# Rotary embedding on one core: one early load moved to SyncE's queue, one late load split in two

## The chip, the core and the metric

The kernel runs on one core of a Trainium2 chip. It uses all five engines of the core: TensorE (PE in the profile), VectorE (DVE), ScalarE (ACT), GpSimd (POOL) and SyncE (SP), and the 16 DMA engines that move data between HBM and SBUF. The metric is the device time of one execution in microseconds.

## The reference

The input `x` has 16 batches of 512 positions with 1024 numbers each, 16 heads of 64. `cos` and `sin` have one row of 32 numbers for each position.

```python
x = x.reshape(batch, seq, num_heads, head_dim)
x1, x2 = x[..., :half_dim], x[..., half_dim:]
cos = cos[None, :, None, :]
sin = sin[None, :, None, :]
rotated = np.concatenate([x1 * cos - x2 * sin, x1 * sin + x2 * cos], axis=-1)
```

For each head, the first half of the result is `x1*cos - x2*sin` and the second half `x1*sin + x2*cos`. All is float32: 33.55 MB are read and as many written.

## The kernel before

The 8192 positions are cut into 64 units, called rows in the code and here, numbered `u` from 0 to 63. A row is a block of 128 partitions by 1024 numbers (512 KB). Eight rows make a tile (4 MB). There are eight tiles, called tile 1 to tile 8 here; the code numbers them from 0. In SBUF there is a ring of 40 rows, so tiles 1 to 5 have places of their own, and tiles 6, 7 and 8 use those of tiles 1, 2 and 3 again. The result is written over the input in SBUF and stored from there.

`TILES` (L33) has one line for each tile: its rows, its place in the ring, into how many loads and stores it is cut, and the stores that must have landed before it may be loaded. Tile 1 is loaded and stored in two halves of four rows, tile 8 is stored in two halves; all else moves in whole tiles. That makes nine loads and ten stores.

Each row takes two products and one sum:

- VectorE multiplies the row by the cosine into PSUM (`t1_ps`, three buffers, L341).
- The row with its halves swapped is multiplied by the signed sine into `t2_sb` (six buffers), mostly by GpSimd: two rows at once at L308, one row at L165. VectorE takes a few of these rows itself (L165).
- The two are summed. For 45 rows VectorE adds them (L350). For 19 rows TensorE adds `t2_sb` into PSUM by a product with the identity (L268), and ScalarE copies the sum to SBUF (L230).

The engines run in written order, each with its own list of instructions, and wait on semaphores. VectorE multiplies row `u` and then adds row `u - 1`. GpSimd goes ahead of VectorE as far as the six buffers allow. On GpSimd and VectorE the wait for a load stands at the first row of that load (`wait_landed`, L190).

The tables: SyncE loads `sin` and `cos` first (L196). TensorE spreads them over the partitions by small matrix products (L251), ScalarE turns them into the sine table (L220, L221), and only then can VectorE and GpSimd begin.

The queues: all loads of `x` are issued by ScalarE. The six loads of tiles 1 to 5 come first, before anything else that ScalarE does (L208). The loads of tiles 6, 7 and 8 are late loads: they stand in ScalarE's list behind rows 21, 28 and 37 (`BEHIND`, L45), and each waits for the stores whose place it takes (L233). SyncE issues the two tables and then the ten stores, each as soon as its last row is summed (`wait_added`, then L203). At the end SyncE waits for the stores that no load waited for (L204).

Of the kernel before, what the change touches and what calls it, by code (L numbers as in the profile page):

```python
# [6 lines left out]
def bass_split_heads_rope_kernel(  # L7
# [21 lines left out]
    COPY = mybir.ActivationFunctionType.Copy  # L29

    TILES = (  # L33
        (8, 0, (4, 4), (4, 4), ()),
        (8, 8, (8,), (8,), ()),
        (8, 16, (8,), (8,), ()),
        (8, 24, (8,), (8,), ()),
        (8, 32, (8,), (8,), ()),
        (8, 0, (8,), (8,), (0, 1)),
        (8, 8, (8,), (8,), (2,)),  # L40
        (8, 16, (8,), (4, 4), (3,)),
    )
    RING = 40

    BEHIND = {6: 21, 7: 28, 8: 37}  # L45
    first_row = [sum(t[0] for t in TILES[:i]) for i in range(len(TILES))]
    NU = sum(t[0] for t in TILES)
    assert NU * P == batch * seq
# [3 lines left out]

    loads = []
    stores = []
    for t, (n, place, ins, outs, _) in enumerate(TILES):
        assert sum(ins) == n == sum(outs) and place + n <= RING
        loads += [(t, sum(ins[:i]), m) for i, m in enumerate(ins)]
        stores += [(t, sum(outs[:i]), m) for i, m in enumerate(outs)]
    load_at = {(t, o): i for i, (t, o, _) in enumerate(loads)}
    store_after = {first_row[t] + o + m - 1: i for i, (t, o, m) in enumerate(stores)}  # L60
    late = [i for i, (t, _, _) in enumerate(loads) if TILES[t][4]]
    awaited = sorted({k for t in TILES for k in t[4]})


    V_ROWS = {8: (3, 6)}
# [25 lines left out]
    with ExitStack() as stack:  # L91
# [13 lines left out]
        sem_in = [stack.enter_context(nc.semaphore(f"in{i}")) for i in range(len(loads))]  # L105
        sem_out = {k: stack.enter_context(nc.semaphore(f"out{k}")) for k in awaited}
# [39 lines left out]
        def in_dram(flat, t, o, m):  # L146
            n = TILES[t][0]
            run = flat[first_row[t] * P:(first_row[t] + n) * P, :].rearrange("(p r) d -> p (r d)", r=n)
            return run[:, o * dim:(o + m) * dim]

        def place_of(u):
            t, r = rows[u]
            return TILES[t][1] + r

        def in_sbuf(t, o, m):
            k = TILES[t][1] + o
            return x_sb[:, k:k + m].rearrange("p n h t d -> p (n h t d)")
# [14 lines left out]
        def wait_added(eng, u):  # L172
            if n_pe[u]:
                eng.wait_ge(sem_a, n_pe[u])
            if n_comb[u]:
                eng.wait_ge(sem_v, n_comb[u])
# [9 lines left out]
        def load(eng, i):  # L186
            t, o, m = loads[i]
            eng.dma_start(in_sbuf(t, o, m), in_dram(xf, t, o, m)).then_inc(sem_in[i], 16)

        def wait_landed(eng, t, r):  # L190
            if (t, r) in load_at:
                eng.wait_ge(sem_in[load_at[t, r]], 16)

        def on_sync(sp):
            for c, table, sem in ((1, sin, sem_sin), (0, cos, sem_cos)):
                sp.dma_start(stage[:, c, :], table.rearrange("(s r) d -> s (r d)", r=R1)).then_inc(sem, 16)  # L196
            for u in range(NU):
                if u not in store_after:
                    continue
                k = store_after[u]  # L200
                t, o, m = stores[k]
                wait_added(sp, u)
                sp.dma_start(in_dram(of, t, o, m), in_sbuf(t, o, m)).then_inc(sem_out.get(k, sem_rest), 16)  # L203
            sp.wait_ge(sem_rest, 16 * (len(stores) - len(awaited)))  # L204

        def on_scalar(ae):
            early = [i for i in range(len(loads)) if i not in late]
            for i in early:  # L208
                load(ae, i)
            ae.wait_ge(sem_i, 2)  # L210
            for n in SIZES:
                m = n // R1
                ae.activation(  # L213
                    pick[n][:],
                    ident[:].rearrange("q (s k) -> q k s", k=m)[:, :, None, :].broadcast_to([P, m, m, P // m]),
                    COPY,
                ).then_inc(sem_g, 1)
            for i, n in enumerate(SIZES):
                ae.wait_ge(sem_t, i + 1)
                ae.activation(s_sb[n][:, :, 0, :], raw_sin[n], COPY, scale=-1.0)  # L220
                ae.activation(s_sb[n][:, :, 1, :], raw_sin[n], COPY).then_inc(sem_s, 1)  # L221
            for n in SIZES:
                v = V_ROWS[n]
                some = raw_sin[n][:, v[0]:v[-1] + 1:max(1, v[-1] - v[0]), :]
                ae.activation(v_ps[n][:, :, 0, :], some, COPY, scale=-1.0)
                ae.activation(v_ps[n][:, :, 1, :], some, COPY).then_inc(sem_s, 1)
            for u in range(NU):
                if PE2[u]:
                    ae.wait_ge(sem_e, n_pe[u])
                    ae.activation(xs[:, place_of(u), :], t1_ps[:, u % NT1, :], COPY).then_inc(sem_a, 1)  # L230
                for i in late:
                    if BEHIND[i] == u:
                        for j in TILES[loads[i][0]][4]:  # L233
                            ae.wait_ge(sem_out[j], 16)
                        load(ae, i)

        def on_tensor(pe):
            pe.wait_ge(sem_z, 1)
            for k in range(NT1):
                for b in range(EH):  # L240
                    pe.matmul(  # L241
                        t1_ps[:, k, b * BANK:(b + 1) * BANK], zero[:, 0:P], zero[:], start=True, stop=True
                    ).then_inc(sem_w, 1)
            pe.wait_ge(sem_g, len(SIZES))
            pe.wait_ge(sem_cos, 16)
            pe.wait_ge(sem_sin, 16)
            pe.wait_ge(sem_w, NT1 * EH)
            for n in SIZES:
                for c, to in enumerate((c_ps[n], raw_sin[n])):
                    for k in range(n // R1):  # L250
                        ins = pe.matmul(  # L251
                            to[:, k * R1:(k + 1) * R1, :].rearrange("p r d -> p (r d)"),
                            pick[n][:, k].rearrange("q b s -> q (b s)"),
                            stage[:, c, :],
                            start=c == 0,
                            stop=True,
                            skip_group_check=c == 1,
                        )
                ins.then_inc(sem_t, 1)
            for u in range(NU):  # L260
                if not PE2[u]:
                    continue
                if TWO[u - 1]:
                    pe.wait_ge(sem_q[(u - 1) % NT2], made[u - 1])
                pe.wait_ge(sem_q[u % NT2], made[u])
                t2 = t2_sb[:, u % NT2, :, :, :].rearrange("p h t d -> p (h t d)")
                for b in range(EH):
                    ins = pe.matmul(  # L268
                        t1_ps[:, u % NT1, b * BANK:(b + 1) * BANK],
                        ident[:],  # L270
                        t2[:, b * BANK:(b + 1) * BANK],
                        start=False,
                        stop=True,
                        skip_group_check=True,
                    )
                ins.then_inc(sem_e, 1)
# [40 lines left out]
        def on_vector(ve):  # L317
# [39 lines left out]
            for u in range(NU + LEAD):  # L357
# [6 lines left out]
                if u >= LEAD and not ahead and not PE2[u - LEAD]:  # L364
                    comb(u - LEAD)

        on_sync(nc.sync)
        on_scalar(nc.scalar)
        on_gpsimd(nc.gpsimd)
        on_tensor(nc.tensor)  # L370
        on_vector(nc.vector)

# [32 lines left out]
```

## Time and profile before

| what | us |
|---|---|
| median of 3 runs | 161.01 (160.85 to 161.12) |
| profiled execution, its own time | 160.98 |
| its span, first to last instruction | 159.7 |
| VectorE busy | 133.8 (84%) |
| GpSimd busy | 126.3 (79%) |
| TensorE busy | 60.5 (38%) |
| ScalarE busy | 22.1 (14%) |
| share of the 16 DMA engines' time, loads of x (q10) | 49.4% |
| the same, tables and stores (q1) | 49.1% |

The span lies between the first and the last instruction of the program; the time of the execution has some more around it. A transfer has two moments in the profile: its issue by SyncE or ScalarE, and its landing, when its semaphore has counted all of its 16 engines. Between the two it may stand in its queue behind earlier transfers. In what follows, a time without more said is counted from the start of the span.

The cost of the instructions on a row:

```profile
L308 POOL TENSOR_TENSOR t_sb<-x_sb,sine 128x2048 f32<-128x2048 f32 x22 | 99.1, 4526 | 1.6 <-DMA x_sb<-in_x_dram 1.3
L341 DVE TENSOR_TENSOR t_ps<-x_sb,tab_ps 128x1024 f32<-128x1024 f32 x64 | 76.8, 1221 | 14.1 <-PE t_ps L251 12.5
L350 DVE TENSOR_TENSOR x_sb<-t_ps,t_sb 128x1024 f32<-128x1024 f32 x45 | 54.5, 1215 | 1.6 <-POOL t_sb L308 0.9
L230 ACT ACTIVATE x_sb<-t_ps 128x1024 f32<-128x1024 f32 x19 | 19.5, 1024 | 91.5 <-PE t_ps L268 91.5
```

Each line has the busy time of the group and the mean duration in ns of one instruction, and behind the second bar the idle time of the engine just before them and what ended most of it.

### The profile page before, as it was taken

The numbers are of one execution on the slowest core, as the hardware profiler recorded it, in microseconds if no ns is written. First come the engines' busy times: TensorE is split into PE (matmuls) and PEld (weight loads), VectorE is DVE, ScalarE is ACT, GpSimd is POOL, SyncE is SP. The second block draws the span as 40 slices with busy tenths as digits, with TensorE's granted clock in tenths as the row PEclk, the third lists the DMA queues.
The fourth block names the chain that finished last, engine by engine and source line by source line (L and its number), as shares of the span: only waits on it lengthen the run. The fifth ranks groups of instructions, "written<-read, shape, count | busy, mean of one in ns | idle before, by whom it ended". The sixth has DMA issues, their size and how long they took to land.

```text
span 159.7 us, 449 instructions
## 1 busy us (share of the span) xinstructions
PE 60.5 (38%) x90; PEld 20.9 (13%) x90; DVE 133.8 (84%) x119; ACT 22.1 (14%) x25; POOL 126.3 (79%) x40
## 2 busy tenths in 40 slices
PE   6013001893540954089509870854098100000000
PEld 1013001130110221023102220211022000000000
DVE  0005897999999999999899989999999899999600
ACT  0302000114220042011500250052002200000000
POOL 1003999999999999999999999999999699940000
PEclk9999999999996599755995576599755955555555
DMA  5999999999998999999999999999999999999896
GB/s 176 440 410 451 443 476 394 394 460 394 394 509 369 501 394 394 501 412 402 451 460 402 418 492 394 402 484 427 402 443 468 394 427 484 402 402 484 373 447 271
DMA packets 3025, 67.25 MB, mean 421 GB/s; under 512 B 336, under 2 KB 592, under 8 KB 592
## 3 DMA queue, kind: packets, MB, share of 16 engines
q10 hardware_dynamic: 1296, 33.56, 49.4%
q1 hardware_dynamic: 1728, 33.69, 49.1%
q14 instruction: 1, 0.01, 0.0%
HBM read 33.69 MB, written 33.55 MB: 421 GB/s over the span
## 4 chain that ended last, share of the span: by engine, by line
DVE 63%; PE 11%; POOL 8%; DMA 6%; ACT 3%; issue 2%; SPq 0%; POOLq 0%
DVE t_ps L341 35%; DVE x_sb L350 23%; PE t_ps L268 9%; DMA stage<-in_cos_dram 6%; DVE t_sb L165 6%; POOL t_sb L165 5%; POOL t_sb L308 3%; ACT x_sb L230 3%; PE tab_ps L251 1%; PE t_ps L251 1%; ACT sine L220 0%; SPq L196 0%; ACT sine L221 0%; POOLq L299 0%
## 5 line engine op out<-in xcount | busy, mean ns | idle before, releaser
L308 POOL TENSOR_TENSOR t_sb<-x_sb,sine 128x2048 f32<-128x2048 f32 x22 | 99.1, 4526 | 1.6 <-DMA x_sb<-in_x_dram 1.3
L341 DVE TENSOR_TENSOR t_ps<-x_sb,tab_ps 128x1024 f32<-128x1024 f32 x64 | 76.8, 1221 | 14.1 <-PE t_ps L251 12.5
L268 PE MATMUL t_ps<-t_sb,ident 128*128 128x512 f32 x76 | 55.7, 881 | 55.1 <-DVE t_ps L341 41.2
L350 DVE TENSOR_TENSOR x_sb<-t_ps,t_sb 128x1024 f32<-128x1024 f32 x45 | 54.5, 1215 | 1.6 <-POOL t_sb L308 0.9
L165 POOL TENSOR_TENSOR t_sb<-x_sb,sine 128x1024 f32<-128x1024 f32 (+1 forms) x12 | 27.3, 2288 | 13.0 <-ACT sine L221 13.0
L230 ACT ACTIVATE x_sb<-t_ps 128x1024 f32<-128x1024 f32 x19 | 19.5, 1024 | 91.5 <-PE t_ps L268 91.5
L268 PEld LDWEIGHTS t_ps<-t_sb,ident 128*128 128x128 f32 x76 | 18.4, 269 | 91.1 <-issue 59.6
L165 DVE TENSOR_TENSOR t_sb<-x_sb,tab_ps 128x1024 f32<-128x1024 f32 (+1 forms) x9 | 10.2, 1135 | 0.0
L251 PE MATMUL tab_ps<-stage,chosen 128*128 128x128 f32 x4 | 1.2, 454 | 7.5 <-DMA stage<-in_cos_dram 7.5
L241 PE MATMUL t_ps<-zero 128*128 128x512 bf16 x6 | 2.7, 627 | 1.2 <-DVE zero L318 1.2
L251 PEld LDWEIGHTS tab_ps<-stage,chosen 128*128 128x128 f32 x4 | 0.9, 322 | 8.4 <-issue 8.4
L213 ACT ACT_TABLE_LOAD x1 | 1.3, 1283 | 3.8 <-issue 3.8
L220 ACT ACTIVATE sine<-t_ps 128x256 f32<-128x256 f32 x1 | 0.4, 384 | 8.1 <-PE t_ps L251 8.1
L251 PE MATMUL t_ps<-stage,chosen 128*128 128x128 f32 x4 | 1.1, 421 | 0.0
L318 DVE MEMSET zero<- 128x256 uint32 x1 | 0.3, 272 | 0.9 <-PEq L387 0.9
L241 PEld LDWEIGHTS t_ps<-zero 128*128 128x128 bf16 x6 | 0.7, 135 | 2.4 <-DVE zero L318 1.2
L251 PEld LDWEIGHTS t_ps<-stage,chosen 128*128 128x128 f32 x4 | 1.0, 333 | 0.0
L279 POOL MEMSET ident<- 128x128 f32 x1 | 0.2, 205 | 0.3 <-POOLq L387 0.3
L213 ACT ACTIVATE chosen<-ident 128x256 f32<-128x256 f32 x1 | 0.4, 430 | 0.0
L221 ACT ACTIVATE sine<-t_ps 128x256 f32<-128x256 f32 x1 | 0.4, 377 | 0.0
L281 POOL TENSOR_SCALAR_AFFINE_SELECT ident<-ident 128x128 f32<-128x128 f32 x1 | 0.3, 293 | 0.1
L387 POOL MEMSET const-float32-0.0<- 128x1 f32 x1 | 0.1, 98 | 0.3 <-issue 0.3
(5 smaller groups left out, 0.7 us busy)
## 6 DMA issues: line engine op xcount, KB each, us to landing
x_sb<-in_x_dram ACTq DMA_DIRECT2D x7, 4096.0 KB, 29.1
out_dram<-x_sb SPq DMA_DIRECT2D x6, 4096.0 KB, 28.5
out_dram<-x_sb SPq DMA_DIRECT2D x4, 2048.0 KB, 15.4
x_sb<-in_x_dram ACTq DMA_DIRECT2D x2, 2048.0 KB, 9.7
stage<-in_sin_dram SPq DMA_DIRECT2D x1, 64.0 KB, 5.5
stage<-in_cos_dram SPq DMA_DIRECT2D x1, 64.0 KB, 10.2
```

The lines of the kernel that those rows point to most:

```text
L165: return eng.tensor_tensor(t2_sb[:, u % NT2, a:b, :, :], swapped(place_of(u))[:, a:b], table[:, None, :, :].broadcast_to([P, b - a, 2, HALF]),
L213: ae.activation(pick[n][:], ident[:].rearrange("q (s k) -> q k s", k=m)[:, :, None, :].broadcast_to([P, m, m, P // m]), COPY,).then_inc(se ...
L220: ae.activation(s_sb[n][:, :, 0, :], raw_sin[n], COPY, scale=-1.0)
L221: ae.activation(s_sb[n][:, :, 1, :], raw_sin[n], COPY).then_inc(sem_s, 1)
L230: ae.activation(xs[:, place_of(u), :], t1_ps[:, u % NT1, :], COPY).then_inc(sem_a, 1)
L241: pe.matmul(t1_ps[:, k, b * BANK:(b + 1) * BANK], zero[:, 0:P], zero[:], start=True, stop=True).then_inc(sem_w, 1)
L251: ins = pe.matmul(to[:, k * R1:(k + 1) * R1, :].rearrange("p r d -> p (r d)"), pick[n][:, k].rearrange("q b s -> q (b s)"), stage[:, c, :] ...
L268: ins = pe.matmul(t1_ps[:, u % NT1, b * BANK:(b + 1) * BANK], ident[:], t2[:, b * BANK:(b + 1) * BANK], start=False, stop=True, skip_group ...
L281: pl.affine_select(out=ident[:], in_=ident[:], compare_op=mybir.AluOpType.is_equal, fill=0.0, base=0, pattern=[[-1, P]], channel_multiplier=1,
L308: pl.tensor_tensor(t2_sb[:, u % NT2:u % NT2 + 2].rearrange("p n h t d -> p (n h) t d"), x_sb[:, k:k + 2, :, ::-1, :].rearrange("p n h t d ...
L341: ve.tensor_tensor(t1_ps[:, u % NT1, :].rearrange("p (h d) -> p h d", d=HALF), x_sb[:, k, :, :, :].rearrange("p h t d -> p (h t) d"), c_ps ...
L350: ve.tensor_tensor(xs[:, place_of(u), :], t1_ps[:, u % NT1, :], t2_sb[:, u % NT2, :, :, :].rearrange("p h t d -> p (h t d)"), add,).then_i ...
```

## The change

- The load of tile 3 (number 3 in the list of loads) is issued by SyncE, behind the two tables and ahead of the stores, and no longer by ScalarE.
- Tile 6 is loaded in two halves of four rows. Its first half waits for the store of rows 0-3 and stands behind row 13; its second half waits for the store of rows 4-7 and stands behind row 21. The load of tile 7 stands behind row 29 (before: 28), that of tile 8 behind row 37 as before. There are ten loads now.
- GpSimd and VectorE wait for both halves of tile 6 at its first row. Neither waits for the first half of tile 1 any more; TensorE does, before the small products that spread the tables.

```diff
     TILES = (
-        (8, 0, (4, 4), (4, 4), ()),
-        (8, 8, (8,), (8,), ()),
...
-        (8, 0, (8,), (8,), (0, 1)),
-        (8, 8, (8,), (8,), (2,)),
-        (8, 16, (8,), (4, 4), (3,)),
+        (8, 0, (4, 4), (4, 4)),
+        (8, 8, (8,), (8,)),
...
+        (8, 0, (4, 4), (8,)),
+        (8, 8, (8,), (8,)),
+        (8, 16, (8,), (4, 4)),
     )
-    BEHIND = {6: 21, 7: 28, 8: 37}
+    FREED_BY = {6: 0, 7: 1, 8: 2, 9: 3}
+    BEHIND = {6: 13, 7: 21, 8: 29, 9: 37}
+
+    ON_SYNC = 3
...
         def wait_landed(eng, t, r):
-            if (t, r) in load_at:
-                eng.wait_ge(sem_in[load_at[t, r]], 16)
+            for i, (v, o, _) in enumerate(loads):
+                if i and v == t and r == (o if t == 0 else 0):
+                    eng.wait_ge(sem_in[i], 16)
...
                 sp.dma_start(stage[:, c, :], table.rearrange("(s r) d -> s (r d)", r=R1)).then_inc(sem, 16)
+            load(sp, ON_SYNC)
...
-            early = [i for i in range(len(loads)) if i not in late]
+            early = [i for i in range(len(loads)) if i not in late and i != ON_SYNC]
...
                     if BEHIND[i] == u:
-                        for j in TILES[loads[i][0]][4]:
-                            ae.wait_ge(sem_out[j], 16)
+                        ae.wait_ge(sem_out[FREED_BY[i]], 16)
                         load(ae, i)
...
             pe.wait_ge(sem_w, NT1 * EH)
+            pe.wait_ge(sem_in[0], 16)
```

More of the change, by code (lines that the diff above doesn't have):

```diff
@@ L33, in bass_split_heads_rope_kernel @@
     TILES = (
-        (8, 0, (4, 4), (4, 4), ()),
-        (8, 8, (8,), (8,), ()),
-        (8, 16, (8,), (8,), ()),
-        (8, 24, (8,), (8,), ()),
-        (8, 32, (8,), (8,), ()),
-        (8, 0, (8,), (8,), (0, 1)),
-        (8, 8, (8,), (8,), (2,)),
-        (8, 16, (8,), (4, 4), (3,)),
+        (8, 0, (4, 4), (4, 4)),
+        (8, 8, (8,), (8,)),
+        (8, 16, (8,), (8,)),
+        (8, 24, (8,), (8,)),
+        (8, 32, (8,), (8,)),
+        (8, 0, (4, 4), (8,)),
+        (8, 8, (8,), (8,)),
+        (8, 16, (8,), (4, 4)),
     )
     RING = 40
-    BEHIND = {6: 21, 7: 28, 8: 37}
+    FREED_BY = {6: 0, 7: 1, 8: 2, 9: 3}
+    BEHIND = {6: 13, 7: 21, 8: 29, 9: 37}
+    ON_SYNC = 3
     first_row = [sum(t[0] for t in TILES[:i]) for i in range(len(TILES))]
@@ L54, in bass_split_heads_rope_kernel @@
     stores = []
-    for t, (n, place, ins, outs, _) in enumerate(TILES):
+    for t, (n, place, ins, outs) in enumerate(TILES):
         assert sum(ins) == n == sum(outs) and place + n <= RING
@@ L58, in bass_split_heads_rope_kernel @@
         stores += [(t, sum(outs[:i]), m) for i, m in enumerate(outs)]
-    load_at = {(t, o): i for i, (t, o, _) in enumerate(loads)}
     store_after = {first_row[t] + o + m - 1: i for i, (t, o, m) in enumerate(stores)}
-    late = [i for i, (t, _, _) in enumerate(loads) if TILES[t][4]]
-    awaited = sorted({k for t in TILES for k in t[4]})
+    late = sorted(FREED_BY)
+    awaited = sorted(FREED_BY.values())
     V_ROWS = {8: (3, 6)}
```

## The prediction

> **What bounds the kernel now.** I read the slices of the span first, then the waits, then the moments at which single transfers were issued and landed.
>
> ```profile
> DVE  0005897999999999999899989999999899999600
> POOL 1003999999999999999999999999999699940000
> DMA  5999999999998999999999999999999999999896
> ```
>
> Three resources run close to full at once. VectorE (DVE) and GpSimd (POOL) are busy from the fourth slice on, and the 16 DMA engines from the first slice to the last. VectorE stops in the third slice from the end (one slice is 4 us): the last 9 us belong to stores. The waits say the same, with the store wait at the end and one wait for a load:
>
> ```profile
> SPq L204 <- DMA out_dram<-x_sb: 8.9, 1, 8.9
> POOL t_sb L308 <- DMA x_sb<-in_x_dram: 1.3, 1, 1.3
> ```
>
> How fast the engines work, and how two queues share them, is in the DMA view of two stretches: 13.2 to 23 us (only the second tile's load runs, on ScalarE's queue, q10), and 43 to 57 us (the second half store on SyncE's queue, q1, beside whole-tile loads on q10). Columns: packets, MB, share.
>
> ```profile
> q10 hardware_dynamic: 144, 4.19, 99.1%
> ...
> q10 hardware_dynamic: 141, 4.10, 67.8%
> q1 hardware_dynamic: 142, 2.10, 35.0%
> ```
>
> 144 packets are 128 pieces, one for each partition and so 8 for each engine, and 16 small ones. In the second stretch both queues sent the same number of packets, though those of q1 are half as large: the engines alternate piece for piece, not byte for byte. Then the issues, one window each (us from issue to landing), in this order: the load of rows 4-7 (issued 1.22), of the second tile (1.71), of the seventh tile (77.36), of the eighth (96.70); the half stores of rows 0-3 (24.20), rows 4-7 (36.84), and the last two (142.59, 150.51).
>
> ```profile
> x_sb<-in_x_dram ACTq DMA_DIRECT2D x1, 2048.0 KB, 12.0
> x_sb<-in_x_dram ACTq DMA_DIRECT2D x1, 4096.0 KB, 21.2
> x_sb<-in_x_dram ACTq DMA_DIRECT2D x1, 4096.0 KB, 29.0
> x_sb<-in_x_dram ACTq DMA_DIRECT2D x1, 4096.0 KB, 29.1
> out_dram<-x_sb SPq DMA_DIRECT2D x1, 2048.0 KB, 18.6
> out_dram<-x_sb SPq DMA_DIRECT2D x1, 2048.0 KB, 20.5
> out_dram<-x_sb SPq DMA_DIRECT2D x1, 2048.0 KB, 12.3
> out_dram<-x_sb SPq DMA_DIRECT2D x1, 2048.0 KB, 9.2
> ```
>
> Issue plus duration gives landings: rows 4-7 at 13.2, second tile 22.9, seventh 106.4, eighth 125.8; stores 42.8, 57.3, 154.9, 159.7. One 4 MB tile alone takes 22.9 - 13.2 = 9.7 us, so 9.7 / 8 = 1.21 us per 32 KB piece and 0.61 per 16 KB piece. Seventh to eighth tile: 19.4 = 2 x 9.7, the load sharing evenly with stores. A half beside whole tiles: 57.3 - 42.8 = 14.5 = 8 x (1.21 + 0.61). So the engines lose nothing in the mix; 16 tiles of traffic are 16 x 9.7 = 155.2 of the 159.7 us. No reordering lowers this floor by itself. VectorE's slack against it is small: its last store, issued at 150.51, queues behind the one landing at 154.9. With about 1 us from issue to first data (my estimate: the first half load took 7.4 us for 8 pieces of 0.61 with tables beside it, so 2.5 us at most lie around the pieces), VectorE may end about 2.9 us later before the engines run dry.
>
> **The change, part by part.** Which work is late, with the rows that show it:
>
> ```profile
> 29.59 4.52 POOL L308 TENSOR_TENSOR t_sb<-x_sb,sine 128x2048 f32<-128x2048 f32 x1
> 35.28 1.21 DVE L350 TENSOR_TENSOR x_sb<-t_ps,t_sb 128x1024 f32<-128x1024 f32 x1
> ...
> 125.86 4.52 POOL L308 TENSOR_TENSOR t_sb<-x_sb,sine 128x2048 f32<-128x2048 f32 x1 [1.28 <-DMA x_sb<-in_x_dram]
> 133.39 1.21 DVE L350 TENSOR_TENSOR x_sb<-t_ps,t_sb 128x1024 f32<-128x1024 f32 x1
> ```
>
> These are GpSimd's product for rows 8, 9 and the add of row 8; then the product for rows 56, 57 (the only load wait) and the add of row 56.
>
> 1. *Tile 3 on SyncE's queue.* Its issue (0.4 us, like the tables') falls in SyncE's idle time before 24.20. Its pieces come after the tables', whose last lands at 1.22 + 10.2 = 11.4. From there until 13.2, three 16 KB pieces of rows 4-7 (1.8 / 0.61) are left, each now followed by a tile-3 piece: rows 4-7 land near 13.2 + 3 x 1.21 = 16.8. GpSimd takes them at 22.81, so 6 us of tile 1's products hide this; without that cover it would cost the 3.6. Then tiles 2 and 3 alternate, two tiles in 19.4 us from 13.2 = 32.6, tile 3 done first by its lead of 3; beside tile 2's last 2-3 pieces go pieces of the half store queued behind tile 3 at 24.20, 2.5 x 0.61 = 1.5. Tile 2 lands at about 34.1 instead of 22.9. Two loads side by side are not in this trace: 22.9 (ScalarE's queue served first) is the lower bound and 34.1 the upper; I take the upper, since load and store do alternate. GpSimd wants it at 29.59: 4.5 late. The add of row 8 wants that product: 34.1 + 4.5 = 38.6 instead of 35.28, so VectorE is 3.3 late. GpSimd is busy without a pause afterwards; VectorE's only spare time is the four waits on ScalarE, 1.6 us in all: 1.7 to 3.4 us late stay at row 56 (133.39 - 3.39 = 130.00 for its multiply, which moves to 131.7-133.4).
>
> 2. *The half loads of tile 6, and all that follows.* One issue more on ScalarE (0.34 us, in its idle 91.5). In the engines it is 8 turns more. Count turns from tile 2 to the landing of tile 8: ScalarE's queue now has 7 transfers (tiles 2, 4, 5, 6a, 6b, 7, 8) and SyncE's gets as many turns: tile 3, the two half stores, and the stores of tiles 2 to 5, 7 transfers, plus a lead of 2-4 pieces, now of tile 6's store. By then 8 tiles are loaded and 5.25 to 5.5 stored: 13.25-13.5. Before, tile 8 landed at 125.8 when 8 were loaded and 4.5 stored (tile 5's store, issued at 99.11 with 31.5 us to landing, lands at 130.6, 4.8 us or half a tile later). So tile 8 is 0.75 to 1.0 tile later, 7.3 to 9.7 us: 133.1 to 135.5, taken at 134.0 because a turn may be lost where a store comes just after its queue emptied.
>
> 3. *What tile 8 holds up.* GpSimd's product of rows 56, 57 starts at 134.0, ends 138.5; the add of row 56 waits for it; from that add (133.39) to VectorE's end (150.44) are 17.1 us without a gap. End of VectorE: 138.5 + 17.1 = 155.6, 5.2 late. This absorbs the lateness of part 1, it isn't added to it: rows up to 55 are done by then. The last store then finds the engines empty. No row has a lone store: 4.85 (154.9 to 159.7, the pieces alone) and 7.4 (the first half load beside the tables) bound it; I take 6.5, nearer the upper since issue and landing must be paid. 155.6 + 0.1 + 6.5 = 162.2.
>
> 4. *Small waits.* TensorE's new wait for rows 0-3 (land 0.80 + 7.4 = 8.2) is hidden behind the cosine table (11.4), 3.2 us of cover; the two waits dropped on GpSimd and VectorE save nothing. ScalarE's waits for stores: the half stores land near 44 and 58, tile 2's store near 75, tile 3's near 90, while the row before each wait (13, 21, 29, 37) is evicted at 45.88, 61.71, 78.03 and 94.73 plus some 3; each is cleared by 5 us or more. Were one missed, evictions of the next rows would queue behind it and VectorE would wait for their PSUM. ScalarE's ring always holds a load (tile 5 lands near 64, tile 6a is issued near 50), so the earlier issues make no load earlier: the queue decides, not the issue. Five early issues instead of six end 0.45 us sooner, in ScalarE's idle 8.07 before the sine.
>
> *Sum:* span 159.7 -> 162.2, +2.5. The profiled execution took 160.98 with a span of 159.7, so 1.28 lie around the span; its time is 0.03 under the median 161.01. That gives 163.5; I forecast 163.4, the lone store being perhaps a little nearer its lower bound.
>
> **The rivals.**
>
> *A. Only the second tile's stall counts.* SyncE's queue runs dry for a few turns (tile 4's store is issued at 82.77 + 3.3 = 86, and tile 3's finishes near 89), so tile 8 lands by 132 and VectorE is late by 3.3 at most: end 153.8, last store 160.4, time 161.7 (161.4 to 162.3). For it: lateness must pass through store issues. Against: the queues were never dry before.
>
> *B. No change.* The lateness stays under the 2.9 us of slack because VectorE wins back its 1.6, and tile 8 lands before 131.5. Then the DMA floor sets the end as now: 161.0. The Trainium skill, DMA: Bandwidth & Descriptors, section on issuing engines not being separate DMA queues, speaks for this: all queues run on the same 16 engines and interleave, so another issuing engine saves sequencer time only. The trace agrees on the bandwidth (9.7 us alone, 19.4 for two tiles shared), but there the order, not the rate, is what changes.
>
> *C. Faster.* The first tile took until 13.2 us for 9.7 us of pieces. If tile 3's pieces are let in among the tables' 512-byte ones, up to 3.5 less the 1.0-1.9 before the first data, some 1.6 us, come back for every later transfer, and the stores end sooner if VectorE is under 1.3 us late: 159.4 to 160.6. Against: they stand behind the tables on the same queue, and tile 2 then lands no sooner.
>
> *D. Worse.* The lead is 5 pieces or more, or tile 3 delays the cosine table: each piece is 1.21; two more give 165.8.
>
> **How the numbers follow.** Forecast 0.57 (162.3 to 165.0), A 0.22, B 0.12, C 0.05, D 0.04. About 0.2% (0.3 us) can be told from no change. Slower: 0.57 + 0.22 + 0.04 = 0.83; same 0.12; faster 0.05. The range leaves out C, D and most of B: 161.1 to 165.0.
>
> **What would show it.** A wait of GpSimd of 4-5 us for a load near 30 us, tile 2 landing near 34; a second one near 129-134, tile 8 landing near 134; VectorE ending near 155-156; DMA with a gap just before the last store; SyncE's wait for the last store near 6.5 instead of 8.9 us. Wrong if tile 2 lands before 30 (the queues don't alternate), if tile 8 lands by 131, or if VectorE ends before 153.4: then A or B holds.

## The result, and the profile after

| | us |
|---|---|
| before, median | 161.01 |
| after, median of 4 runs | 162.86 (162.45 to 163.25) |
| ratio | 1.0115, 95% interval 1.0089 to 1.0142 |
| profiled execution after, its span | 163.25, 162.0 |

The change makes the kernel 1.2% slower. The forecast was 163.4.

The slices of the span after (4 us each), then the waits (total us, times, longest):

```profile
DVE  0005897954999999999989998999999989899940
POOL 1004999339999999999999999999899919999000
DMA  5999999999999999999999999899998998998947
```

```profile
POOL t_sb L314 <- DMA x_sb<-in_x_dram: 9.6, 3, 5.4
...
DVE x_sb L356 <- POOL t_sb L314: 3.6, 3, 2.2
DVE t_ps L347 <- DMA x_sb<-in_x_dram: 1.9, 1, 1.9
DVE t_ps L347 <- ACT x_sb L236: 1.7, 4, 0.4
...
SPq L210 <- DMA out_dram<-x_sb: 6.0, 1, 6.0
```

New are a hole in GpSimd in slices 8 and 9 (28 to 36 us) and one in VectorE in slices 9 and 10 (32 to 40 us), a dent in GpSimd near 130 us, and one in the DMA row just before the end (the 4 in slice 39). GpSimd waits for loads three times, 9.6 us in all, where it waited once for 1.3. The last store is awaited 6.0 us instead of 8.9. The timeline has the places (start, duration, idle before it):

```profile
35.23 4.51 POOL L314 TENSOR_TENSOR t_sb<-x_sb,sine 128x2048 f32<-128x2048 f32 x1 [5.44 <-DMA x_sb<-in_x_dram]
...
114.61 4.51 POOL L314 TENSOR_TENSOR t_sb<-x_sb,sine 128x2048 f32<-128x2048 f32 x1 [0.60 <-DMA x_sb<-in_x_dram]
...
133.99 4.51 POOL L314 TENSOR_TENSOR t_sb<-x_sb,sine 128x2048 f32<-128x2048 f32 x1 [3.59 <-DMA x_sb<-in_x_dram]
```

```profile
39.77 1.22 DVE L356 TENSOR_TENSOR x_sb<-t_ps,t_sb 128x1024 f32<-128x1024 f32 x1 [2.22 <-POOL t_sb L314]
...
138.54 1.23 DVE L356 TENSOR_TENSOR x_sb<-t_ps,t_sb 128x1024 f32<-128x1024 f32 x1 [0.50 <-POOL t_sb L314]
...
153.25 2.35 DVE L356 TENSOR_TENSOR x_sb<-t_ps,t_sb 128x1024 f32<-128x1024 f32 x2
```

These are GpSimd's products for rows 8-9, 48-49 and 56-57, and VectorE's adds of rows 8, 56 and 62-63. The add of row 8 starts 4.5 us later than before (35.28), VectorE ends 5.2 us later (155.6 instead of 150.4). The transfers behind it, one window each: tile 3 (issued at 1.70 by SyncE), tile 2 (at 1.71), tile 8 (99.25), the last store (155.67).

```profile
x_sb<-in_x_dram SPq DMA_DIRECT2D x1, 4096.0 KB, 27.6
x_sb<-in_x_dram ACTq DMA_DIRECT2D x1, 4096.0 KB, 33.5
x_sb<-in_x_dram ACTq DMA_DIRECT2D x1, 4096.0 KB, 34.7
out_dram<-x_sb SPq DMA_DIRECT2D x1, 2048.0 KB, 6.3
```

Issue plus duration: tile 3 lands at 29.3, tile 2 at 35.2 (before: 22.9), tile 8 at 133.9 (before: 125.8), the last store at 162.0.

### The profile page after: what moved, and what is told of

It reads as the page before. It is cut to its first block, busy times and chain, and to the rows that moved or that the text cites. A ratio compares the mean times of both kernels' runs of the same rounds, so it can differ in the third digit from the quotient of the medians.

```text
span 162.0 us, 449 instructions
## 1 busy us (share of the span) xinstructions
PE 63.9 (39%) x90; PEld 21.8 (13%) x90; DVE 134.1 (83%) x119; ACT 22.1 (14%) x25; POOL 126.3 (78%) x40
## 4 chain that ended last, share of the span: by engine, by line
DMA 42%; DVE 37%; PE 9%; POOL 6%; ACT 1%; issue 1%; ACTq 1%
DMA x_sb<-in_x_dram 42%; DVE t_ps L347 19%; DVE x_sb L356 14%; PE t_ps L274 9%; POOL t_sb L314 6%; DVE t_sb L167 3%; ACT x_sb L236 1%; ACTq L190 1%
## 5 line engine op out<-in xcount | busy, mean ns | idle before, releaser
L274 PE MATMUL t_ps<-t_sb,ident 128*128 128x512 f32 x76 | 59.1, 930 | 56.1 <-DVE t_ps L347 38.5
L274 PEld LDWEIGHTS t_ps<-t_sb,ident 128*128 128x128 f32 x76 | 19.3, 281 | 94.6 <-issue 44.8
```

What stands on the lines that cost most here:

```text
L274: ins = pe.matmul(t1_ps[:, u % NT1, b * BANK:(b + 1) * BANK], ident[:], t2[:, b * BANK:(b + 1) * BANK], start=False, stop=True, skip_group ...
```

## The experiments

Three theories were put against each other. Theory 1: tile 2's late landing and tile 8's late landing each suffice to end above the floor of the DMA engines, and they overlap. Theory 2: only the late tile 2 counts. Theory 3: only the late tile 8 counts, VectorE having won the first delay back. All ratios are to the kernel before.

### One part alone: tile 3 on SyncE's queue

```diff
-        (8, 0, (4, 4), (8,)),
+        (8, 0, (8,), (8,)),
...
-    FREED_BY = {6: 0, 7: 1, 8: 2, 9: 3}
-    BEHIND = {6: 13, 7: 21, 8: 29, 9: 37}
+    FREED_BY = {6: (0, 1), 7: (2,), 8: (3,)}
+    BEHIND = {6: 21, 7: 28, 8: 37}
...
```

> Only the first part of the change: SyncE loads tile 3, tile 6 stays whole. Tile 2 should land near 35 as in the changed kernel, so GpSimd waits some 5.4 us and VectorE is some 4.5 us late from row 8 on. Tile 8 should land by 129, before GpSimd wants it. Theory 1 (late tile 2 and late tile 8 each suffice, and overlap): VectorE ends near 155.1, span 161.2 to 161.5, time 162.5 to 162.8. Theory 2 (only the late tile 2 counts): the same. Theory 3 (only the late landing of tile 8 counts, VectorE wins the first delay back): span 159.7 to 160.2, time 161.0 to 161.5.

Measured: 162.57 us, ratio 1.0096 by the medians (interval 1.007 to 1.013), span 161.2. The timeline of GpSimd has one wait for a load, and VectorE's last line is:

```profile
35.10 4.51 POOL L315 TENSOR_TENSOR t_sb<-x_sb,sine 128x2048 f32<-128x2048 f32 x1 [5.41 <-DMA x_sb<-in_x_dram]
...
152.45 2.35 DVE L357 TENSOR_TENSOR x_sb<-t_ps,t_sb 128x1024 f32<-128x1024 f32 x2
```

VectorE ends at 154.8, 4.4 us late, though tile 8 is in time. Its add of row 8 starts at 39.64, 4.4 us late too, so nothing is won back in the rows between. Theory 3 falls. The medians do not tell this kernel (162.01 to 163.18) from the changed one (162.45 to 163.25): that tile 8 costs something on top of tile 2 in the changed kernel is seen in its profiled execution alone, where VectorE ends 0.8 us later than here.

### The other part alone: tile 6 in halves

```diff
-    ON_SYNC = 3
+    ON_SYNC = None
...
-            load(sp, ON_SYNC)
```

> Only the second part: tile 6 in halves, rows 13 to 37, all loads on ScalarE's queue. Tile 2 lands near 23 as before, no wait near 30. Tile 8 gets 8 more turns of stores ahead of it: 134 to 135.5. Theories 1 and 3: VectorE ends 155.6 to 157, span 162 to 163.5, time 163.3 to 164.8. Theory 2 (tile 8's landing costs nothing): time 161.0 to 161.3.

Measured: 167.04 us, ratio 1.038 (1.033 to 1.043), span 165.6. This is more than any theory gave. Theory 2 falls with it. GpSimd now waits for tile 6, tile 7 and tile 8 in turn:

```profile
97.94 4.51 POOL L313 TENSOR_TENSOR t_sb<-x_sb,sine 128x2048 f32<-128x2048 f32 x1 [5.86 <-DMA x_sb<-in_x_dram]
...
118.21 4.51 POOL L313 TENSOR_TENSOR t_sb<-x_sb,sine 128x2048 f32<-128x2048 f32 x1 [4.48 <-DMA x_sb<-in_x_dram]
...
137.58 4.51 POOL L313 TENSOR_TENSOR t_sb<-x_sb,sine 128x2048 f32<-128x2048 f32 x1 [3.58 <-DMA x_sb<-in_x_dram]
```

Tile 8 lands at 137.5, 2.0 us past the expected 134 to 135.5. The parts do not add: +1.5 and +6.0 alone, +1.85 together.

### Tile 2 in tile 3's place, with the halves

```diff
-    ON_SYNC = 3
+    ON_SYNC = 2
```

> The changed kernel with tile 2 instead of tile 3 on SyncE's queue: tile 2 now has the lead and lands near 29.3, tile 3 near 35, in time for its row 16 at 45. The wait near 30 is gone, tile 8 still lands at 131.5 to 134. Theory 1: only the wait for tile 8 is left, VectorE ends 153 to 155.6, span 160 to 162, time 161.3 to 163.2. Theory 2: time 161.0 to 161.3. Theory 3: as the changed kernel, 162.5 to 163.2.

Measured: 164.85 us, ratio 1.0255 (1.020 to 1.031), span 163.8. The wait near 30 us is gone, as expected, and the kernel is *slower* than the changed one by 2.0 us. No theory said so. GpSimd waits 3.2, 4.7 and 3.6 us for tiles 6, 7 and 8; in the changed kernel it waits 0.6 for tile 7 and 3.6 for tile 8. Tile 8 lands at 135.8, not 133.9. The DMA view of the stretch from 86.5 to 92.3 us shows why. First the changed kernel, then this one (packets, MB, share; q1 is SyncE's queue, q10 ScalarE's):

```profile
q1 hardware_dynamic: 60, 1.44, 57.7%
q10 hardware_dynamic: 91, 1.29, 52.1%
```

```profile
q1 hardware_dynamic: 63, 1.54, 62.0%
q10 hardware_dynamic: 64, 1.05, 42.2%
```

With tile 2 on SyncE's queue the two queues sent packet for packet. In the changed kernel the loads sent 31 packets more than the stores, about two on each of 16 engines. There the rows were late, so tile 4's store was issued at 87.3 (with tile 2 on SyncE's queue: 82.4), only some 2 us before tile 3's store ended. SyncE's queue ran dry, and the load of tile 6 took its turns. The changed kernel from 88.97 to 90.8 us:

```profile
q10 hardware_dynamic: 48, 0.79, 100.2%
q1 hardware_dynamic: 16, 0.00, 0.5%
```

The loads sent 48 pieces, three for each engine, and the stores nothing but the 16 small packets that mark the end of tile 3's store. Two of the three took turns that stores would have had, 2 x 1.21 = 2.4 us. On 15 engines tile 6 is indeed that much earlier: its landing marks lie at 92.4 to 92.7 us, with tile 2 on SyncE's queue at 94.8 to 95.2. The late tile 2 costs VectorE 4.5 us and gives part of it back, because late stores let the loads go ahead.

Of the three theories the first is left, and only in kind: a late tile 2 is enough by itself, and so are the late landings behind the halves, but there the tops of its ranges lie 2.2 and 1.65 us under the measured times.

### Tile 2 on SyncE's queue, tile 6 whole

Tile 6 whole as in the first experiment, with `ON_SYNC = 2` as in the third.

> Tile 2 on SyncE's queue and tile 6 whole: neither tile 2 nor tile 8 should be late. All three theories: the floor of the DMA engines as before, time 160.8 to 161.3. Slower than that would mean that a load on SyncE's queue has a cost of its own, by the same rate of the engines.

Measured: 161.25 us, ratio 1.0015 (1.0006 to 1.0024), no wait for a load. With both landings in time the kernel is back within 0.2% of the kernel before. A load on SyncE's queue costs almost nothing by itself (0.2 us); what cost 1.5 us in the first experiment is which tile stands there.

### Halves against halves

Tile 6 in halves, all loads on ScalarE's queue, and the store of tile 3, which runs beside them, in halves too.

```diff
     TILES = (
...
-        (8, 16, (8,), (8,)),
+        (8, 16, (8,), (4, 4)),
...
-    FREED_BY = {6: 0, 7: 1, 8: 2, 9: 3}
+    FREED_BY = {6: (0,), 7: (1,), 8: (2,), 9: (3, 4)}
...
-    ON_SYNC = 3
+    ON_SYNC = None
...
```

> The halves of tile 6 alone cost +6.0 us. Theory: the DMA engines take the two queues piece for piece, so a load cut into 16 KB pieces gives whole-tile stores (32 KB pieces) 8 extra turns. If so, cutting the store of tile 3, which runs beside it, into halves too takes these turns back: by the count of turns tile 8 lands when 4.4 tiles are stored (before: 4.5), near 125, GpSimd waits for no load, and the time is 161.0 to 161.4. Rival: a late load suffers from its halves as such (one more issue, one more wait for a store, both halves awaited at row 40): then the time stays near 167.

Measured: 161.06 us, ratio 1.0001 (0.9992 to 1.0011). The whole 6.0 us are gone; GpSimd waits 0.6 us for one load. The DMA view from 75 to 88.5 us, first with halves of the load alone, then of the store too:

```profile
q1 hardware_dynamic: 122, 3.70, 63.9%
q10 hardware_dynamic: 135, 1.95, 33.7%
```

```profile
q1 hardware_dynamic: 198, 2.98, 51.6%
q10 hardware_dynamic: 195, 2.83, 49.0%
```

With pieces of 16 KB against 32 KB the load moved 1.95 MB while the stores moved 3.70; with equal pieces, 2.83 against 2.98. That the engines take the two queues piece for piece is shown; that halves cost something as such is refuted.

### Three late loads issued four rows later

```diff
-    BEHIND = {6: 13, 7: 21, 8: 29, 9: 37}
+    BEHIND = {6: 17, 7: 25, 8: 29, 9: 41}
```

> The changed kernel with three of the late loads issued four rows later (behind rows 17, 25, 29, 41). Theory: ScalarE's queue always holds an earlier load at these moments, so the issue moves nothing and the time stays at 162.4 to 163.3. Rival: the landing follows the issue: each load some 8 to 10 us later, GpSimd waits as long at rows 40 and 56, time 168 or more.

Measured: 164.17 us, ratio 1.017 (1.012 to 1.022), 1.3 us over the changed kernel, though one of the four runs (162.96) lies among the changed kernel's. Both sides miss, the rival by far. The first two moves cost nothing that the trace shows (GpSimd waits at neither row 40 nor row 48), but tile 8, issued at 108.5 while tile 7 landed at 112.7, lands at 134.9 with a wait of 5.25 us. The DMA view from 111 to 113 us:

```profile
q1 hardware_dynamic: 28, 0.92, 123.1%
q10 hardware_dynamic: 6, 0.10, 11.5%
```

Now it is ScalarE's queue that is dry. The first engines had finished tile 7 by 110.5, and tile 8's first piece moves at 112.9, 4.4 us after its issue. Tile 8's first landing mark comes 21.8 us after tile 7's, in the changed kernel 19.4. So an issue 2 us ahead of the first engines' last piece was too late here, while the first two moves left the issue far enough ahead.

### A shorter last store

The last store of four rows is cut in two of two rows, in the changed kernel and in the kernel before.

```diff
-        (8, 16, (8,), (4, 4)),
+        (8, 16, (8,), (4, 2, 2)),
```

> The changed kernel with the last store cut in two of two rows each (stores of 4, 2 and 2 rows). Theory: the 2.0 us over the floor are the DMA engines waiting empty for the last four rows. Rows 60, 61 can go out near 152.3 and the last 1 MB takes 2.4 us of pieces instead of 4.9: span 159.6 to 160.3, time 160.9 to 161.6. Rival (the lateness lies in the engines' total of bytes or in their turns): stays near 162.9.

> The kernel before with the same cut of its last store. Theory: the DMA engines have work without a break until the end, so a shorter last store changes nothing: 160.8 to 161.3. If the kernel before also ends on VectorE, it gets faster by up to 2.4 us.

Measured: 161.96 us for the changed kernel (ratio 1.005, 1.003 to 1.007), 0.9 us faster than without the cut; 160.99 for the kernel before (0.9996, 0.9987 to 1.0005). The wait for the last store in the changed kernel with the cut:

```profile
SPq L210 <- DMA out_dram<-x_sb: 3.5, 1, 3.5
```

3.5 instead of 6.0 us: the cut saves 2.5 us behind VectorE's end, as worked out. The profiled run gave 1.4 of it back, since its tile 8 landed at 135.2 and not at 133.9, though the two kernels are the same up to the last stores. Three of the eight runs (161.52 to 161.56) are in the expected 160.9 to 161.6; that the others miss it for the same reason was not seen. The kernel before does not gain, since its DMA engines have work until the end.

## Why the prediction was right, point by point

- *Floor.* Right. The kernel before, with a shorter last store, stays at 160.99; two other orders of the loads give 161.06 and 161.25. No order tried beats it.
- *Tile 2 late.* Right in kind, mis-sized by 1.1: it lands at 35.2 and not 34.1, and the add of row 8 is 4.5 late and not 3.3. Rows 4-7 landed at 17.1 and not 16.8, and from 29.2 to 35.2 us the stores' queue sent 64 pieces, four for each engine, where 2.5 were taken; these are 0.3 and 0.9 us.
- *VectorE wins back up to 1.6 us from its waits on ScalarE.* Wrong. These waits stay (1.7 us after, 1.6 before), and with tile 3 alone the delay is 4.4 at row 8 and 4.4 at the end. Rival A had carried its 3.3 us to the end without this gain. The first experiment, where as in rival A only the second tile's stall counts, measured 162.57 and not 161.7 because of the 1.1 us above.
- *Tile 8 at 134.0.* It landed at 133.9, but the hit is in part luck. SyncE's queue lost two turns on 15 engines, where the prediction took one for possible, and these engines were done by 131.5, before its range of 133.1 to 135.5; one slow engine made it 133.9 (see the end). Where SyncE's queue was not seen dry, the count is nearer: 133.5 to 134.1 on 15 engines and 135.8 on the last in the third experiment. With the halves alone it falls short (137.5). One term is missing in it: the second half brings not only 8 pieces for each engine but a mark as well. From 80 to 86.5 us both queues of the changed kernel sent 59 packets, 11 of the loads' being marks, so a mark takes a turn, beside whole pieces 1.2 us. The rest of that gap stays open.
- *What tile 8 holds up.* Right to 0.1: from GpSimd's product of rows 56-57 to VectorE's end are 21.6 us in the changed kernel (133.99 to 155.6), with halves alone (137.58 to 159.2) and with tile 2 on SyncE (135.83 to 157.4). That it absorbs the first delay is right too, but with only 0.5 us of VectorE's time to spare, where the prediction's own numbers leave 1.7 to 3.4 (138.5 less 133.39 and the lateness of part 1).
- *The lone store.* 6.5 was taken from issue to landing; it took 6.3.
- *The small waits.* Right: each late load is issued within 0.01 us of the start of the eviction ahead of it (49.93, 65.85, 82.55, 99.25). That the issue never matters is wrong near the end of the queue, as the run with later rows shows.
- *The sum.* Span 162.0 for 162.2. The profiled execution, 163.25, is the slowest of the four; the forecast of 163.4 is 0.5 above the median. The number alone proves little: the first experiment, without a late tile 8, measured 162.57, inside the forecast's 162.3 to 165.0 too.

What the prediction did not see is that its two delays work on each other. The halves alone cost 6.0 us. With tile 2 in time on SyncE's queue they cost 3.8; why that queue takes off 2.2 was not tested. The late tile 2 takes off 2.0 more, since it makes the rows late that would wait for the late loads anyway, and holds back the stores that push the loads aside. So of the 5.2 us by which VectorE ends late, tile 2 brings 4.4 by itself, and tile 8, which set the end in the forecast, the last 0.8.

## What to carry to other kernels

In these runs, where two queues were full, the engines took them piece for piece, so the size of a transfer's pieces set its share: cutting a load that is needed soon into smaller pieces gave its bandwidth to the other queue (1.95 MB beside 3.70), and cutting the other side alike took it back. Count turns to the landing, not bytes, and count the marks. In the kernel before the DMA engines never rested, and none of the orders tried beat it; what an order could do was make the last transfer start late. Before adding up the costs of two edits, ask whether one delays what the other one waits for.

## What the runs showed of the hardware

The 16 engines of a transfer need not stay together. In the changed kernel tile 8's landing marks lie between 131.1 and 131.5 us on 15 engines and at 133.9 on one. The DMA view from 131.6 to 133.8 us:

```profile
q1 hardware_dynamic: 32, 1.05, 110.3%
q10 hardware_dynamic: 1, 0.00, 0.0%
```

In 2.2 us the loads' queue sent one packet of a few bytes, the last mark, and the stores 32 whole pieces: GpSimd stood still for it. The slow engine had moved its last piece of tile 8 from 131.1 to 132.4, then a store's piece, then the mark. In the kernel before the marks were 0.9 us apart (124.9 to 125.8). The marks of earlier transfers show where the gap grows: the last mark is 0.7 us behind the other 15 at tile 3's store (90.34 against 89.66), 1.9 at tile 6's second half (94.63 against 92.73) and 2.4 at tile 7 (114.54 against 112.10). Between the first two SyncE's queue was dry. By the times of the packets, put end to end, 15 engines moved three pieces of the load before the new store's first piece; the one that was behind still had the old store's piece to move and got two, so it was a piece of the load behind from then on. Whether this is also why the changed kernel's times scatter by 0.8 us over four runs (0.5 over 23 of the kernel before) was not tested. Why one engine falls behind first stays open.
